# First feed-forward layer of a two-layer trunk: 288, 256 and 272 columns for its three matmul parts

## The chip, the cores and the metric

The kernel runs on one core of one Trainium2 chip. TensorE multiplies matrices, VectorE, ScalarE and GpSimd do the element-wise work, and SyncE issues the transfers. The metric is the time of one execution on the device, in microseconds.

## The reference

The reference is a decoder trunk of two layers with model width 2048 over 272 positions: 16 learned meta tokens and a sequence of 256. What matters here is the feed-forward part, once in each layer:

```python
def rmsnorm(x, g):
    y = x * lax.rsqrt(jnp.mean(x * x, axis=-1, keepdims=True) + EPS)
    return y * g

def conv_ffn(h, w_up, dw, w_down):          # D_FF = 5632
    u = causal_dwconv(h @ w_up, dw)         # width 3, causal, per channel
    val, gate = u[..., :D_FF], u[..., D_FF:]
    return (jax.nn.silu(gate) * val) @ w_down

for i in range(2):
    h = h + mixer_i(rmsnorm(h, norm_mix[i]))
    h = h + conv_ffn(rmsnorm(h, norm_ffn[i]), w_up[i], dw[i], w_down[i])
return rmsnorm(h, norm_final)[:, 16:]
```

The mixer of layer 0 is two convolution branches with a common output projection, that of layer 1 a gated linear attention and a recurrence. All inputs are float32.

## The kernel before

Positions lie along the free axis, so `h` is 16 tiles of 128 channels by 272 positions, and a matrix product for 128 output channels is a loop over k steps of 128 input channels each.

Every large product goes through `gemm_steps` (line 151). A product's weights come from memory in pieces of 8 k steps (`wf`, line 155). For 4 k steps at a time ScalarE makes the high part `wh` of the weights (line 161, a float32r cast), and VectorE (GpSimd in some products of the first mixer) the low part `wl`, what the cast left over (line 163). The moving operand is split in the same way into `xh` and `xl`. A k step is three matmuls into the same accumulator: `wh` with `xh`, `wh` with `xl`, `wl` with `xh` (lines 181 to 183). There is a second form (lines 169 to 179), used where `xs` holds triples: the positions whose low part is not multiplied apart lie in front of `xh` as additional columns, copied there from `xl`. `wh` then meets a wide operand (copied low columns, then `xh`), and the rest of `xl` in a second, narrower matmul; the accumulator's columns of the copied part are added to where they belong afterwards. In the kernel before the second form is used in the up products of layer 1 alone, with 2 such columns: 260, 256 and 258 columns. There the wide operand of the last k step is the product's last matmul.

`Norm` (line 208) makes the operand for the next products: `make_x` writes `xh` (ScalarE), `xl` (VectorE) and, where wanted, the copied columns (GpSimd, line 228) into rows of `XW` = 320 columns for the feed-forward norms and layer 0 and of 272 for the mixer of layer 1; `feed` adds up the squares, `finish` makes `rstd`, by which a product's result is multiplied afterwards.

`ffn` (line 431) runs two halves. In each, 22 pairs of up products (16 k steps each) give `val` and `gate`: the result times `rstd` into `u` (line 452), a convolution over three positions (`conv3`: ScalarE, then twice VectorE), a SiLU, a product on GpSimd (line 459), and the split into `act` (line 462), 22 tiles with rows of 320 columns in layer 0. Then 16 down products of 22 k steps each add to `h` (line 465). In layer 0 all of these have 272 columns. The tile `gap` (line 434) has no content; it shifts what is allocated behind it.

The mixer of layer 0, `mixer_ab` (line 275), ends in an output projection in two parts of 16 products with 8 k steps each (lines 415 to 427), the first over `s_split`, whose last entry is made at lines 372 to 377. In between, a layer norm written as a generator (`ln_gen`) is moved on by one step after each product. After it comes `ffn` of layer 0, the mixer of layer 1 (`mixer_cd`), `ffn` of layer 1, and the output: `ob` is scaled on VectorE and GpSimd and stored in eleven pieces from SyncE (lines 1091 to 1097). `omm` and `omka` (lines 1060 and 1061) are small constants for the mixer of layer 1, computed from the parameters on VectorE; the order on an engine is the order that the scheduler gives to instructions that don't depend on each other.

## Time and profile before

| | |
|---|---|
| median of 3 runs | 2460.76 us (2458.37, 2460.76, 2470.93) |
| the profiled execution | 2459.09 us |
| span of the profiled execution | 2457.3 us |
| TensorE busy | 2427.9 us (99%), 20476 matmuls |
| VectorE, ScalarE, GpSimd busy | 1794.0, 1338.9, 571.6 us |
| transfers | 53.0% of the 16 engines' time on the main queue |

The profile is one execution. TensorE (PE) is busy nearly all the time; VectorE is DVE, ScalarE ACT, GpSimd POOL and SyncE SP in its rows. The printed duration of a matmul is from its start to its end, and successive matmuls overlap; how far apart they start is read from their starts. The stages in order of time: mixer of layer 0 to 349 us, up and down products of layer 0 in two halves to 1132, mixer of layer 1 to 1702, up and down products of layer 1 to 2443, output.

### The profile page before, as it was taken

The numbers are of one execution on the slowest core, as the hardware profiler recorded it, in microseconds if no ns is written. First come the engines' busy times: TensorE is split into PE (matmuls) and PEld (weight loads), VectorE is DVE, ScalarE is ACT, GpSimd is POOL, SyncE is SP. The second block draws the span as 40 slices with busy tenths as digits, with TensorE's granted clock in tenths as the row PEclk, the third lists the DMA queues.
The fourth block names the chain that finished last, engine by engine and source line by source line (L and its number), as shares of the span: only waits on it lengthen the run. The fifth ranks groups of instructions, "written<-read, shape, count | busy, mean of one in ns | idle before, by whom it ended". The sixth has DMA issues, their size and how long they took to land.

```text
span 2457.3 us, 53575 instructions
## 1 busy us (share of the span) xinstructions
PE 2427.9 (99%) x20476; PEld 2371.8 (97%) x20476; DVE 1794.0 (73%) x3400; ACT 1338.9 (54%) x2573; POOL 571.6 (23%) x894
## 2 busy tenths in 40 slices
PE   8999999999999999999999999999999999999998
PEld 8999999999999999999999988899999999999997
DVE  8897897776556777667786678879777755777754
ACT  5444665555445555546745445546555545555653
POOL 5776140000000000121248044416110000101122
PEclk9999999999999999999999999999999999999999
DMA  6555555555665555665446342345555566555564
GB/s 223 191 176 180 172 173 180 181 178 173 181 183 179 178 177 180 181 196 190 142 148 179 126 130 84 101 131 179 188 184 188 183 191 197 187 184 186 179 198 147
DMA packets 130991, 423.95 MB, mean 173 GB/s; under 512 B 18832, under 2 KB 27216, under 8 KB 130736
## 3 DMA queue, kind: packets, MB, share of 16 engines
q1 hardware_dynamic: 129824, 417.99, 53.0%
q8 instruction: 161, 2.64, 0.4%
q0 software_dynamic: 912, 2.55, 0.4%
q14 instruction: 94, 0.77, 0.1%
HBM read 414.41 MB, written 5.93 MB: 171 GB/s over the span
## 4 chain that ended last, share of the span: by engine, by line
PE 97%; DVE 1%; ACT 0%; DMA 0%; issue 0%; POOL 0%; SPq 0%; DVEq 0%; POOLq 0%
PE acc L181 24%; PE acc L183 23%; PE acc L182 23%; PE acc L176 7%; PE acc L175 7%; PE acc L174 6%; PE ps L924 1%; PE ps L958 1%; PE ps L939 0%; PE acc L178 0%; PE ps L973 0%; PE ps L826 0%; PE ps L981 0%; PE ps L987 0%; DVE wl L163 0%
## 5 line engine op out<-in xcount | busy, mean ns | idle before, releaser
L161 ACT CAST wh<-wf 128x512 fp32r<-128x512 f32 (+1 forms) x1576 | 956.3, 611 | 876.4 <-PE acc L182 610.0
L163 DVE TENSOR_TENSOR wl<-wf,wh 128x512 fp32r<-128x512 f32 (+1 forms) x1465 | 1030.2, 708 | 462.6 <-ACT wh L161 417.0
L181 PE MATMUL acc<-x,wh 128*128 128x272 f32 (+2 forms) x2438 | 711.3, 292 | 1.4 <-ACT wh L161 1.4
L183 PE MATMUL acc<-x,wl 128*128 128x272 f32 (+2 forms) x2438 | 700.3, 287 | 1.0 <-DVE wl L163 0.9
L182 PE MATMUL acc<-x,wh 128*128 128x272 f32 (+2 forms) x2438 | 698.7, 287 | 0.0
L181 PEld LDWEIGHTS acc<-x,wh 128*128 128x128 f32 x2438 | 459.4, 188 | 15.7 <-issue 7.6
L183 PEld LDWEIGHTS acc<-x,wl 128*128 128x128 f32 x2438 | 459.7, 189 | 3.2 <-DVE wl L163 1.9
L182 PEld LDWEIGHTS acc<-x,wh 128*128 128x128 f32 x2438 | 459.9, 189 | 1.1 <-issue 0.3
L182 PE MATMUL acc<-act,wh 128*128 128x272 f32 (+1 forms) x1408 | 396.0, 281 | 0.0
L183 PE MATMUL acc<-act,wl 128*128 128x272 f32 (+1 forms) x1408 | 396.0, 281 | 0.0
L181 PE MATMUL acc<-act,wh 128*128 128x272 f32 (+1 forms) x1408 | 396.0, 281 | 0.0
L174 PE MATMUL acc<-x,wh 128*128 128x260 f32 x1144 | 323.6, 283 | 0.0
L176 PE MATMUL acc<-x,wl 128*128 128x258 f32 x1144 | 321.8, 281 | 0.0
L175 PE MATMUL acc<-x,wh 128*128 128x256 f32 x1144 | 321.0, 281 | 0.0
L181 PEld LDWEIGHTS acc<-act,wh 128*128 128x128 f32 x1408 | 264.7, 188 | 0.0
L183 PEld LDWEIGHTS acc<-act,wl 128*128 128x128 f32 x1408 | 264.7, 188 | 0.0
L182 PEld LDWEIGHTS acc<-act,wh 128*128 128x128 f32 x1408 | 264.7, 188 | 0.0
L175 PEld LDWEIGHTS acc<-x,wh 128*128 128x128 f32 x1144 | 215.6, 188 | 0.0
L174 PEld LDWEIGHTS acc<-x,wh 128*128 128x128 f32 x1144 | 215.5, 188 | 0.0
L176 PEld LDWEIGHTS acc<-x,wl 128*128 128x128 f32 x1144 | 215.3, 188 | 0.0
L163 POOL TENSOR_TENSOR wl<-wf,wh 128x512 fp32r<-128x512 f32 x111 | 149.0, 1350 | 55.9 <-ACT wh L161 54.8
L451 POOL MEMSET u<- 128x2 f32 x88 | 8.6, 101 | 572.9 <-DVE c L272 566.3
(334 smaller groups left out, 3740.5 us busy)
## 6 DMA issues: line engine op xcount, KB each, us to landing
wf<-up SPq DMA_DIRECT2D x352, 512.0 KB, 3.5
wf<-down SPq DMA_DIRECT2D x128, 512.0 KB, 3.8
wf<-cd_in SPq DMA_DIRECT2D x100, 512.0 KB, 3.6
wf<-ab_in SPq DMA_DIRECT2D x76, 512.0 KB, 3.6
wf<-down SPq DMA_DIRECT2D x64, 384.0 KB, 3.2
wf<-ab_out_s SPq DMA_DIRECT2D x16, 512.0 KB, 3.5
wf<-ab_out_a SPq DMA_DIRECT2D x16, 512.0 KB, 3.6
wf<-cd_out_o SPq DMA_DIRECT2D x16, 512.0 KB, 3.5
```

Of the source, the lines that this page charges most:

```text
L161: last_hi[0] = S.copy(wh[:, :ns * P], src)
L163: lo = eng.tensor_sub(wl[:, :ns * P], src, wh[:, :ns * P].bitcast(F32))
L174: PE.matmul(acc, a, x4, start=kk == 0, stop=False)
L175: PE.matmul(acc[:, 4:], a, x0, start=False, stop=False)
L176: PE.matmul(acc[:, 2:], b, x2, start=False, stop=False)
L181: PE.matmul(acc, a, xh, start=kk == 0, stop=False)
L182: PE.matmul(acc, a, xl, start=False, stop=False)
L183: PE.matmul(acc, b, xh, start=False, stop=kk == kt - 1)
L451: G.memset(u[:, 0:2], 0.0)
L924: PE.matmul(gv[:, :128], bkc, t[r, h0], start=True, stop=True)
L958: PE.matmul(wy[H[h0], 0:64], t[:, h0, 0:64], sv[:, h0], start=True, stop=True)
```

## The change

In layer 0's feed-forward part both products take the second form, with all 16 meta positions as the copied columns: 16 low columns, then the 272 high ones, make 288 for `wh`; 256 low ones; 272 high ones for `wl`. `make_x` copies 16 columns for `norm_ffn0`, and `act` gets its copy in `ffn`. The result has 288 columns: for an up product it is multiplied by `rx` (`rstd` with its first columns once more in front) into `u`, and GpSimd adds columns 0 to 15 to columns 16 to 31 and then sets two to zero for the convolution; for a down product VectorE adds the first 16 columns to `h` in a second addition. `apart` cuts the three operands so that all end at the end of a row of 320. The accumulator gets 288 columns, `gap` grows from 48 to 80.

Three further edits: the first three products of the output projection of layer 0 are interleaved (four k steps of the first and of the second, then their other four, then the third), `rstd` goes into `cv` ahead of the last product there, and `ln_gen` yields once more; `omm` and `omka` are ordered behind the last weight step of layer 0; the last stores are regrouped, and those of GpSimd's pieces are issued from ScalarE's queue.

```diff
--- before.py
+++ after.py
@@ -36,7 +36,7 @@
 TP = 320
 PAD = 48
 ACT_W = (320, 256)
-ACT_GAP = 48
+ACT_GAP = 80
 XW = 320
 NXW = KD * T // XW
 OUT = NM - 2
@@ -169,11 +169,12 @@
                     if len(xs[kk]) == 3:
 
                         x4, x0, x2 = xs[kk]
+                        e = x2.shape[-1] - SEQ
                         last = kk == kt - 1
                         if not last:
                             PE.matmul(acc, a, x4, start=kk == 0, stop=False)
-                        PE.matmul(acc[:, 4:], a, x0, start=False, stop=False)
-                        PE.matmul(acc[:, 2:], b, x2, start=False, stop=False)
+                        PE.matmul(acc[:, 2 * e:], a, x0, start=False, stop=False)
+                        PE.matmul(acc[:, e:], b, x2, start=False, stop=False)
                         if last:
                             PE.matmul(acc, a, x4, start=False, stop=True)
                         continue
@@ -184,7 +185,7 @@
                 yield
 
     def gemm(w, g, xs, n, pool_lo=()):
-        acc = psA.tile([P, T], F32, tag="acc", name="acc")
+        acc = psA.tile([P, T + 16], F32, tag="acc", name="acc")
         for _ in gemm_steps(w, g, xs, len(xs), acc[:, :n], pool_lo):
             tick()
         return acc[:, :n]
@@ -195,6 +196,10 @@
 
     def parts(t, c0, c1):
         return t[:, 0, c0:c1], t[:, 1, c0:c1]
+
+    def apart(x, n):
+        o = XW - n
+        return x[:, 0, o - (n - SEQ):], x[:, 1, XW - SEQ:], x[:, 0, o:]
 
 
     h = []
@@ -210,6 +215,7 @@
             self.g, self.c0, self.n, self.pool, self.wide = gname, c0, T - c0, pool, gname != "norm_mix1"
             self.ta, self.tb = tags
             self.x, self.acc, self.ps, self.rstd = [], None, None, None
+            self.e = {"norm_ffn0": 16, "norm_ffn1": 2}.get(gname, 0)
 
         def make_x(self, m):
             hm = h[m][:, self.c0:]
@@ -220,12 +226,13 @@
             if self.wide and m >= NXW:
                 slab, i = self.slab2, m - NXW
             x = slab[:, 2 * w * i:2 * w * (i + 1)].rearrange("p (a t) -> p a t", a=2)
-            o = XW - self.n if self.c0 else 0
+            e = self.e
+            o = XW - self.n if e else 0
             xh, xl = parts(x, o, o + self.n)
             S.activation(xh, hm, AF.Copy, scale=pc(self.g, m))
             V.scalar_tensor_tensor(xl, hm, pc(self.g, m), xh.bitcast(F32), op0=ALU.mult, op1=ALU.subtract)
-            if self.c0:
-                G.tensor_copy(x[:, 0, o - 2:o], xl[:, 0:2].bitcast(F32))
+            if e:
+                G.tensor_copy(x[:, 0, o - e:o], xl[:, 0:e].bitcast(F32))
             self.x.append(x)
 
         def feed(self, m):
@@ -252,14 +259,10 @@
             r = npool.tile([P, T], F32, tag="rstd", name="rstd", bufs=2)
             inv_sqrt(r[:, self.c0:], self.ps[:, :self.n], 1.0 / D, "eps")
             self.rstd = r[:, self.c0:]
-            if self.c0 and self.wide:
-                V.tensor_copy(r[:, self.c0 - 2:self.c0], r[:, self.c0:self.c0 + 2])
-                self.rstd = r[:, self.c0 - 2:]
 
         def xs(self):
-            if self.c0:
-                o = XW - self.n
-                return [(x[:, 0, o - 2:], x[:, 1, o + 2:], x[:, 0, o:]) for x in self.x]
+            if self.e:
+                return [apart(x, self.n) for x in self.x]
             return [parts(x, 0, self.n) for x in self.x]
 
     def add_h(m, acc, c0):
@@ -369,9 +372,9 @@
                     V.tensor_mul(up[:, 2:T + 2], u, u2)
                     cv = tp.tile([P, T], F32, tag="t2", name="cv")
                     conv3(cv, up, T, "sc_dw", i)
+                    V.tensor_mul(cv, cv, nm.rstd)
             sb = tp.tile([P, T], F32, tag="t3", name="sb")
-            V.tensor_mul(sb, ps3[2], nm.rstd)
-            V.tensor_mul(sb, sb, cv)
+            V.tensor_mul(sb, ps3[2], cv)
             d = halves[:, i]
             split(d, sb, T)
             s_split.append(parts(d, 0, T))
@@ -395,6 +398,7 @@
                     (G if i % 2 else V).tensor_add(csum, csum, sq)
                 if i % 2:
                     yield
+            yield
             pv = psb()
             PE.matmul(pv[:, :T], ones, csum, start=True, stop=True)
             yield
@@ -412,8 +416,15 @@
 
         ln = ln_gen()
         next(ln, None)
+        accs = [psA.tile([P, T + 16], F32, tag="acc", name="acc")[:, :T] for _ in range(2)] + [psb()[:, :T]]
+        heads = [gemm_steps(A["ab_out_s"], m, s_split, 8, accs[m]) for m in range(3)]
+        for i in (0, 1, 0, 1):
+            next(heads[i])
         for m in range(KD):
-            acc = gemm(A["ab_out_s"], m, s_split, T)
+            if m == 2:
+                for _ in heads[2]:
+                    pass
+            acc = accs[m] if m < 3 else gemm(A["ab_out_s"], m, s_split, T)
             h[m] = hpool.tile([P, T], F32, tag="h", name="h")
             V.tensor_add(h[m], h0[:, m], acc)
             next(ln, None)
@@ -433,10 +444,11 @@
         c0 = nm.c0
         tp.tile([P, ACT_GAP], F32, name="gap", bufs=1)
         n = T - c0
-        pad = 2 if layer == 0 else 0
+        e = nm.e
         no = n if layer == 0 else n - 2
-        ex = 0 if layer == 0 else 2
+        u0 = e - 2 if layer == 0 else e
         xs = nm.xs()
+        rx = tp.tile([P, T + 16], F32, name="rx", bufs=1)[:, :n + e]
         up, down, dw = A["up%d" % layer], A["down%d" % layer], "ffn_dw%d" % layer
         for half in range(2):
             act = []
@@ -444,25 +456,36 @@
                 i = half * NFH + j
                 res = []
                 for q in range(2):
-                    ps = gemm(up, 2 * i + q, xs, n + ex)
-                    nm.finish()
+                    ps = gemm(up, 2 * i + q, xs, n + e)
+                    if nm.rstd is None:
+                        nm.finish()
+                        V.tensor_copy(rx[:, 0:e], nm.rstd[:, 0:e])
+                        V.tensor_copy(rx[:, e:], nm.rstd)
                     u = tp.tile([P, T + 16], F32, tag="u%d" % q, name="u")
-                    if pad:
-                        G.memset(u[:, 0:2], 0.0)
-                    V.tensor_mul(u[:, pad:pad + n + ex], ps, nm.rstd)
-                    if ex:
-                        G.tensor_add(u[:, 2:4], u[:, 2:4], u[:, 0:2])
+                    V.tensor_mul(u[:, :n + e], ps, rx)
+                    G.tensor_add(u[:, e:2 * e], u[:, e:2 * e], u[:, 0:e])
+                    if layer == 0:
+                        G.memset(u[:, u0:e], 0.0)
                     c = tp.tile([P, T], F32, tag="c%d" % q, name="c")
-                    conv3(c[:, :no], u[:, ex:], no, dw, q * NF + i)
+                    conv3(c[:, :no], u[:, u0:], no, dw, q * NF + i)
                     res.append(c[:, :no])
                 silu = S.activation(res[1], res[1], AF.Silu)
                 G.tensor_mul(res[0], res[0], res[1])
-                d = tp.tile([P, 2, ACT_W[layer]], F32R, tag="act", name="act", bufs=24)
-                split(d, res[0], no)
-                act.append(parts(d, 0, no))
+                w = ACT_W[layer]
+                d = tp.tile([P, 2, w], F32R, tag="act", name="act", bufs=24)
+                split(d[:, :, w - no:], res[0], no)
+                if no > SEQ:
+                    G.tensor_copy(d[:, 0, w - no - e:w - no], d[:, 1, w - no:w - SEQ].bitcast(F32))
+                    act.append(apart(d, no))
+                else:
+                    act.append(parts(d, 0, no))
             warm(AF.Sqrt, [silu])
+            ea = no - SEQ
             for m in range(KD):
-                add_h(m, gemm(down, half * KD + m, act, no), T - no)
+                acc = gemm(down, half * KD + m, act, no + ea)
+                add_h(m, acc[:, ea:], T - no)
+                if ea:
+                    V.tensor_add(h[m][:, 0:ea], h[m][:, 0:ea], acc[:, 0:ea])
                 if half:
                     feed(nxt, m)
                     if spill is not None:
@@ -1057,8 +1080,11 @@
 
     omm = cpool.tile([P, 26], F32, name="omm")
     omka = cpool.tile([P, 16], F32, name="omka")[:, :8]
-    V.tensor_scalar(omm, par[:, PO["mu"]:PO["mu"] + 26], -1.0, 1.0, op0=ALU.mult, op1=ALU.add)
-    V.tensor_scalar(omka, par[:, PO["ka"]:PO["ka"] + 8], -1.0, 1.0, op0=ALU.mult, op1=ALU.add)
+    late = last_lo[0]
+    o1 = V.tensor_scalar(omm, par[:, PO["mu"]:PO["mu"] + 26], -1.0, 1.0, op0=ALU.mult, op1=ALU.add)
+    o2 = V.tensor_scalar(omka, par[:, PO["ka"]:PO["ka"] + 8], -1.0, 1.0, op0=ALU.mult, op1=ALU.add)
+    for o in (o1, o2):
+        behind(o, [late])
     with tc.tile_pool(name="cd", bufs=2) as tp:
         nm = mixer_cd(tp, nm)
     with tc.tile_pool(name="ffn1", bufs=2) as tp:
@@ -1088,13 +1114,13 @@
             PE.matmul(ps[:, P * i:P * i + P], rw[:, i], cc("ident", P), start=True, stop=True)
         rs = tp.tile([P, SEQ], F32, name="rs", bufs=1)
         S.copy(rs, ps[:, :SEQ])
-        for a, b in ((0, 1), (1, 2), (11, 12), (2, 4), (12, 13), (4, 6), (13, 14), (6, 8), (14, 15), (8, 11), (15, 16)):
+        for a, b in ((0, 1), (11, 12), (1, 3), (12, 13), (3, 5), (13, 14), (5, 7), (14, 15), (7, 9), (15, 16), (9, 11)):
             for m in range(a, b):
                 if m < 11:
                     V.tensor_mul(ob[:, m], ob[:, m], ps[:, :SEQ])
                 else:
                     G.tensor_mul(ob[:, m], ob[:, m], rs)
-            nc.sync.dma_start(A["outT"][:, a:b], ob[:, a:b])
+            (nc.sync if a < 11 else nc.scalar).dma_start(A["outT"][:, a:b], ob[:, a:b])
```

## Rows read from the trace of the kernel before

**Rows 1.** The page: busy time, share, instructions; granted clock in 40 slices.

```profile
PE 2427.9 (99%) x20476; PEld 2371.8 (97%) x20476; DVE 1794.0 (73%) x3400; ACT 1338.9 (54%) x2573; POOL 571.6 (23%) x894
...
PEclk9999999999999999999999999999999999999999
```

**Rows 2.** By stretch: us, busy (x instructions) of each engine; clock, DMA share, GB/s.

```profile
349.00:609.00 260.00, 260.00 (x2109) 259.92 (x2108) 185.92 (x331) 145.03 (x265) 20.83 (x68) 1.00 0.54 177
...
1000.00:1132.00 132.00, 132.00 (x1085) 131.36 (x1087) 87.99 (x134) 67.38 (x118) 28.04 (x30) 1.00 0.67 192
...
1702.00:1952.00 250.00, 250.00 (x2105) 249.94 (x2104) 187.39 (x331) 149.10 (x265) 25.38 (x66) 1.00 0.56 184
```

**Rows 3.** TensorE by line, six stretches: count, ns min/median/max, first, last start.

```profile
L181 PE MATMUL acc<-x,wh x556: 285/288/288, 745.8 to 997.8; 128*128 128x272 f32 x186
...
L181 PE MATMUL acc<-lt,wh x128: 285/285/288, 745.1 to 994.1; 128*128 128x272 f32 x128
...
L181 PE MATMUL acc<-act,wh x309: 285/285/288, 610.8 to 724.7; 128*128 128x272 f32 x155
...
L181 PE MATMUL acc<-act,wh x340: 276/276/276, 1954.7 to 2070.0; 128*128 128x256 f32 x170
...
L175 PE MATMUL acc<-x,wh x548: 276/281/284, 1710.1 to 1949.9; 128*128 128x256 f32 x183
...
L175 PE MATMUL acc<-lt,wh x126: 276/281/284, 1712.6 to 1946.9; 128*128 128x256 f32 x126
...
L181 PE MATMUL acc<-ysp,wh x121: 281/283/287, 1657.0 to 1700.2; 128*128 128x258 f32 x121
...
L181 PE MATMUL acc<-x,wh x46: 283/288/291, 1274.0 to 1290.9; 128*128 128x272 f32 x46
```

**Rows 4.** TensorE's waits in two stretches: engine line <- releaser: us, times, longest.

```profile
PE ps L251 <- DVE sum L307: 2.1, 1, 2.1
...
PE acc L182 <- DVE halves L194: 1.9, 1, 1.9
```

**Rows 5.** Timeline of VectorE, 28 to 31 us: start, us, engine line op.

```profile
28.50 1.25 DVE L1060 TENSOR_SCALAR omm<-par 128x26 f32<-128x26 f32 x1
...
29.74 1.50 DVE L307 TENSOR_TENSOR sum<-sum,sum 128x272 f32<-128x272 f32 x1
```

**Rows 6.** Timeline of VectorE, 251 to 257 us.

```profile
251.11 0.44 DVE L373 TENSOR_TENSOR sb<-acc,rstd 128x272 f32<-128x272 f32 x1 [0.20 <-PE acc L183]
...
252.29 1.01 DVE L374 TENSOR_TENSOR sb<-sb,cv 128x272 f32<-128x272 f32 x1
...
253.22 1.93 DVE L391 TENSOR_TENSOR conv<-conv,mu 128x272 f32<-128x272 f32 x2
...
255.07 0.99 DVE L194 TENSOR_TENSOR halves<-sb,halves 128x272 fp32r<-128x272 f32 x1
```

**Rows 7.** The tail: timeline of VectorE and GpSimd, and the stores.

```profile
2447.48 3.73 DVE L1094 TENSOR_TENSOR ob<-ob,ps 128x256 f32<-128x256 f32 x11 [1.41 <-ACT rs L1090]
...
2447.53 3.46 POOL L1096 TENSOR_TENSOR ob<-ob,rs 128x256 f32<-128x256 f32 x5 [8.68 <-ACT rs L1090]
...
L1097 SPq DMA_DIRECT2D outT<-ob x11: 343/400/448, 2448.3 to 2453.1; - x11
...
DMA to landing us min/median/max: 1.7/2.2/2.7
```

**Rows 8.** Groups by form of the nearest small operations: busy, mean ns, idle.

```profile
L454 POOL TENSOR_TENSOR u<-u 128x2 f32<-128x2 f32 x88 | 18.4, 209 | 475.1 <-DVE u L452 475.1
...
L228 POOL CAST x<-x 128x2 fp32r<-128x2 f32 x13 | 8.4, 646 | 0.7 <-DVE x L226 0.7
...
L266 DVE TENSOR_TENSOR h<-h,acc 128x272 f32<-128x272 f32 x48 | 20.6, 429 | 0.5 <-PE acc L183 0.5
```

**Rows 9.** Timeline at the first half's last `act`: VectorE and TensorE.

```profile
614.40 0.44 DVE L194 TENSOR_TENSOR act<-c,act 128x272 fp32r<-128x272 f32 x1 [1.99 <-ACT act L193]
...
617.43 0.28 PE L181 MATMUL acc<-act,wh 128*128 128x272 f32 x1
```

## The prediction, made before the change was run

> **What bounds the kernel now.** I read the page's first part, then the clock row, then the waits of TensorE, then the stages one by one. [rows 1]: TensorE is busy for 2427.9 of 2457.3 us and its granted clock is the upper of its two levels, 2.4 GHz, from end to end, so no clock is to be won back. [rows 2]: in the stretch of the first feed-forward layer's up projection TensorE is busy 260.00 of 260.00 us while VectorE has 186 and GpSimd 21; the second layer's up projection, where the form of matmul that the change brings in already stands, looks the same (250.00 of 250.00, GpSimd 25). So in these stages the time is the number of matmuls times the distance from one matmul's start to the next one's. The printed duration of a matmul (0.28 us) is no help, since they overlap; the distance is.
>
> I take the distance from rows that give a count with the first and the last start [rows 3]. One k step is three matmuls (weights high with x high, high with x low, low with x high), and one line holds one of the three, so the distance between two instructions of that line is a k step:
> - layer 0 up, three times 272 columns: (997.8 - 745.1) / 683 = 370.0 ns (556 + 128 instructions);
> - layer 0 down, also 272: (724.7 - 610.8) / 308 = 369.8;
> - layer 1 down, three times 256: (2070.0 - 1954.7) / 339 = 340.1;
> - layer 1 up, 260, 256 and 258 columns: (1949.9 - 1710.1) / 673 = 356.3 (548 + 126);
> - the second half of the output projection of layer 1, three times 258: (1700.2 - 1657.0) / 120 = 360.0;
> - the input projection of layer 1, three times 272, from a slab 272 wide: (1290.9 - 1274.0) / 45 = 375.6, plus or minus 2 as the starts are rounded to 0.1 us.
>
> Only few places make TensorE wait: 2.1 us for the sum of squares at the beginning and 1.9 us for `halves` before the output projection of layer 0 [rows 4]. And behind the last matmul there is a tail in which the output is scaled and stored [rows 7].
>
> **The change, part 1: the matmuls.** A k step of layer 0 keeps its three matmuls and its 816 columns: 3 x 272 becomes 288 + 256 + 272. At 2.4 GHz 816 columns are 340 ns, and [rows 3] show 370.0, so 30 ns of each k step are something else, and the question is whether the new shapes carry less of it. In clock periods (0.4167 ns) a 272 matmul takes 296, which is 272 + 24; a 256 matmul takes 272, which is 256 + 16. I tried a simple rule on the rows: 16 periods for each matmul, and 8 more for each stretch of 64 columns (256 bytes) that its moving operand covers only in part (a piece under 8 columns counts as 8). Rows of 320 = 5 x 64 columns, as `x` and `act` have here, start on such a stretch. The rule is my estimate, made on two of the rows; the other three test it. Input projection of layer 1: the slab's width of 272 puts starts at 0, 16, 32 and 48 within a stretch, half of the steps take 896 periods and half 904, together 375.0 ns (row: 375.6). 258 columns: 868 periods, 361.7 ns (row: 360.0). Layer 1 up: 260 from column 60 and 258 from column 62 end on a stretch and take 288 each, 256 from column 64 takes 272; 848 periods, 353.3 ns (row: 356.3). So the three rows lie 0.6 above, 1.7 below and 3.0 above the rule.
>
> For the new k step: 288 columns from column 32 are half a stretch and four whole ones, 288 + 24 = 312; the 256 from column 64 are four whole ones, 272; the 272 from column 48 are 296. Sum 880 periods, 366.7 ns, or 3.3 below the present 370.0. Layer 0 has 88 up products of 16 k steps (1408) and 32 down products of 22 (704): 2112 x 3.33 ns = **7.0 us gained**. By the rule's own misses the k step may be 365.0 to 369.7, so 10.6 down to 0.6 us. I take the 7.0: the row with the largest miss has pieces of 2 and 4 columns, and the new pieces are 16 and 32, as in the input projection where the rule holds.
>
> A rule that speaks against this part: the Trainium skill (TensorE: Matmul & The Clock Gate, section "Wait — 56ns, not 53.3ns?") gives a warm matmul its columns at 2.4 GHz plus a fixed 2.5 ns or so. By that, equal columns cost equal time and part 1 is worth nothing. The trace does not agree in the step that matters: from 256 to 272 columns a matmul grows by 10.0 ns [rows 3], where that rule would give 6.7.
>
> **Part 2: the work around the matmuls.** All of it lies beside a TensorE that is full, and I cost it at nothing. Each of the 88 up products gains one GpSimd add of 16 columns (0.21 us in its two-column form), in front of the convolution on ScalarE; each of the 44 pairs one GpSimd cast of 16 columns (0.65 us for two) [rows 8]. A pair of products lasts 2 x 16 x 0.37 = 11.8 us, of which GpSimd now fills 0.95 (20.83 us for 22 pairs [rows 2]) and then some 2. ScalarE now waits for that add before the convolution, and behind it are queued the weight casts; layer 1 has this wait already, with TensorE at 250.00 of 250.00 [rows 2]. The 32 down products gain a VectorE add of 16 columns, bounded by the 0.43 us of the 272 form [rows 8], in 8.1 us each. The place with least cover is the last `act` of a half: it is complete at 614.84 and TensorE comes to its first matmul on it at 617.43 [rows 9]. The new chain adds the GpSimd add (0.2) and a memset of two columns before the convolution and the cast (0.65) behind the split, about 1 us of 2.6. Were that cover gone, the cost would be the excess, twice. In the new form the matmul that reads the copied columns is also the last of its product. The norm's 16 new casts (0.65 us each) run during the output projection, before the 5.5 us in which the first up product gets to its last k.
>
> **Part 3: moved steps.** (a) `omm` and `omka` stand in VectorE's queue between the sums of squares and the last sum for which TensorE waits. They hold the queue from 28.50 to 29.74 [rows 5], and the last sum ends at 31.24, which is where TensorE goes on. Sent behind the last weight step of layer 0, they leave 1.24 us: **1.2 us gained**. There VectorE has idle time (88.0 of the 132 us of that stretch busy [rows 2]), and their readers come later. (b) Before the layer-0 output projection TensorE stops for 1.9 us at k 7, as `halves` comes at 256.06 [rows 6]. The change does four more k steps first (1.5 us), and takes `rstd` into `cv` beforehand, so that the 1.01 us product goes out of the chain and the 0.44 us one does both. 1.5 + 1.0 is more than 1.9, and next late is nothing that the waits show: **1.9 us gained**, with 1.5 if VectorE's two `conv` subtractions (1.93 us [rows 6]) still come in between. The weight transfers on SyncE keep their order, one a product; only the second product's is wanted 1.5 us sooner, and its casts on ScalarE and VectorE with it. The additional step in the layer norm's generator moves one small matmul by one product and costs nothing. (c) The tail: the eleven stores go out one behind the other on SyncE, the first at 2448.3 and the last at 2453.1, 0.48 us apart, while VectorE is done at 2451.21 and GpSimd at 2450.99 [rows 7]. With five of them on ScalarE's queue, which is idle then, the last leaves SyncE 0.4 us after VectorE's last multiply, about 2451.6 in place of 2453.1; it carries 256 KB in place of 128, and landings take 1.7 to 2.7 us [rows 7]. So **1.5 us gained**, with bounds 0 (if ScalarE's issues, which the trace doesn't show, take turns with SyncE's) and 1.7.
>
> The sum: 7.0 + 1.2 + 1.9 + 1.5 = 11.6 us. The profiled execution took 2459.1 us as a whole, 1.8 around its span, and the median of the runs is 2460.8. That gives 2447.5 on the one and 2449.2 on the other; I forecast 2448.6.
>
> **The rivals.**
> - *Columns alone count.* The 30 ns beside the columns belong to the three instructions and not to their shapes, and the k step stays within 1 ns of 370. For: the total of columns is the same, and layer 1 up lies 3.0 above my rule, which would nearly undo the 3.3. Against: 256 to 272 grows by 10 ns. Only part 3 is left: 2460.8 - 4.6 = 2456, some 2454 to 2458. The Trainium skill's rule cited above would have it so.
> - *Slower: the mixed form has a price of its own.* Between matmuls of unequal width and operand start, each step may lose time that uniform ones don't. Layer 1 up carries 356.3 ns for 774 columns, 0.4603 a column; at that rate 816 columns take 375.6, or 5.6 more than now, 11.8 us over 2112 steps, less 4.6 from part 3: 2468. It decides from 372.2 ns for a k step, where part 3 is eaten up. Against: that row is still 3.7 below three times 258.
> - *More than forecast.* If a piece at the front of an operand costs nothing because it ends on a whole stretch, each matmul takes its columns + 16: 864 periods, 360.0 ns, 21 us gained, 2435 in all. Against: layer 1 up would be at 342.5, not 356.3.
> - *The change doesn't reach the down products.* `act` lies behind tiles whose sizes change; if its rows began 48 columns off a stretch, the first matmul would have 8 periods more, the second 16, the third 8: 912, 380 ns, 7.0 us lost over 704 steps where 2.3 was to be won. With 4.7 won in the up products and 4.6 in part 3 that is 2458.5. Against: the gap grows by 32 and a tile of 288 comes in, together 320, five whole stretches.
>
> **How the numbers follow.** Forecast 0.55 (2446 to 2451), columns alone 0.22, slower 0.09, more 0.07, down products not reached 0.07. Half a per cent (12.3 us, to 2448.5 or 2473) is about what a measurement of this kernel can tell from no change, and the forecast lies on that edge: I give two fifths of it (0.22) and all of "more" to faster, and add 0.05 for terms that are each a little larger; of the slower case, 0.05 reaches 2473. So faster 0.34, same 0.61, slower 0.05. The range takes in the forecast, "columns alone" and the down case, and leaves out the slower case and most of "more": 2443 to 2459.
>
> **What would show it.** The distance of the line with the 288 columns should be 366.7 ns in both stages of layer 0; TensorE's waits should lose the entry for `halves` and 1.2 us of that for the sum; the last store should leave by 2451.7. A k step above 370, a wait of TensorE for `act` at the head of a down product, or one for the copied columns of `x`, would make the prediction wrong.

## The result: 0.7% slower, and the profile after

| | before | after |
|---|---|---|
| median of 6 runs each, beside one another | 2460.47 us (2458.37 to 2470.93) | 2478.88 us (2477.19 to 2480.22) |
| ratio, 95% interval | | 1.0072 [1.0061, 1.0084] |
| span of the profiled execution | 2457.3 us | 2477.3 us |

The change costs 15 to 21 us where a gain of 12 was forecast; the time lies above the range. First the page of the kernel after: its busy times and the granted clock, as in [rows 1].

```profile
PE 2448.2 (99%) x20476; PEld 2391.0 (97%) x20476; DVE 1809.4 (73%) x3435; ACT 1343.4 (54%) x2573; POOL 604.7 (24%) x1042
...
PEclk9999999999999999999999999999999999999999
```

As many matmuls as before, the upper clock level throughout, and TensorE is busy 20.3 us longer while the span grew by 20.0. So it isn't waiting: its matmuls stand further apart. The first matmul of each stage says where:

| stage | starts at, before | after | length, before | after |
|---|---|---|---|---|
| layer 0 up, first half | 348.72 | 348.17 | 260.94 | 267.55 |
| layer 0 down, first half | 609.66 | 615.72 | 130.24 | 133.65 |
| layer 0 up, second half | 739.90 | 749.37 | 260.48 | 267.23 |
| layer 0 down, second half | 1000.38 | 1016.60 | 132.30 | 136.03 |
| mixer of layer 1 | 1132.68 | 1152.63 | | |

The four stages whose matmuls were changed lose 6.6 + 3.4 + 6.8 + 3.7 = 20.5 us. The mixer of layer 1 (569.0 us up to its feed-forward part) and layer 1's up products (251.4) are as long as before. In the profile the loss is read from the line of the 256-column matmul, which stands once in every k step (the columns are line, operation, count, ns min/median/max, first and last start). The line in a down stage, then in an up stage:

```profile
L176 PE MATMUL acc<-act,wh x316: 279/283/283, 620.0 to 739.6; 128*128 128x256 f32 x158
```

```profile
L176 PE MATMUL acc<-x,wh x546: 279/283/283, 755.6 to 1009.1; 128*128 128x256 f32 x182
L176 PE MATMUL acc<-lt,wh x127: 281/283/283, 754.8 to 1009.9; 128*128 128x256 f32 x127
```

(739.6 - 620.0) / 315 = 379.7 ns and (1009.9 - 754.8) / 672 = 379.6, where [rows 3] had 370.0. Over 2112 k steps 9.7 ns are 20.5 us, the whole loss. A settled k step in the middle of a product takes 380 (starts to the nanosecond). A stretch of the timeline (start, us, engine, line) shows how a k step divides:

```profile
500.84 0.28 PE L176 MATMUL acc<-x,wh 128*128 128x256 f32 x1
500.96 0.29 PE L177 MATMUL acc<-x,wl 128*128 128x272 f32 x1
501.08 0.30 PE L175 MATMUL acc<-x,wh 128*128 128x288 f32 x1
501.22 0.28 PE L176 MATMUL acc<-x,wh 128*128 128x256 f32 x1
```

In starts to the nanosecond, from a matmul's start to the next one's, the 256 takes 118.1, the 272 127.9 and the 288 133.3 (means over 245 us of the first up stage); before, each of the three took 123.3.

The work beside the matmuls stays hidden. The first up stage of layer 0 by window (columns as in [rows 2]):

```profile
350.00:615.00 265.00, 265.00 (x2096) 264.92 (x2096) 191.59 (x330) 147.11 (x262) 35.54 (x129) 1.00 0.52 173
```

TensorE is busy for 265.00 of 265.00 us with GpSimd at 35.54 instead of 20.83. Of the waits of [rows 4] both are gone. What stands there now (TensorE from 20 to 350 us; us, times, longest) is new except for the 0.5 us, which the kernel before has as well:

```profile
PE acc L184 <- DVE wl L163: 1.4, 1, 1.4
PE acc L182 <- ACT wh L161: 0.9, 1, 0.9
PE ps L184 <- DVE wl L163: 0.5, 1, 0.5
PE acc L184 <- POOL wl L163: 0.2, 1, 0.2
```

And the tail, against [rows 7]:

```profile
2467.84 3.73 DVE L1120 TENSOR_TENSOR ob<-ob,ps 128x256 f32<-128x256 f32 x11 [1.72 <-ACT rs L1116]
```

```profile
L1123 SPq DMA_DIRECT2D outT<-ob x6: 332/344/717, 2468.3 to 2471.6; - x6
L1123 ACTq DMA_DIRECT2D outT<-ob x5: 338/380/893, 2468.6 to 2471.4; - x5
...
DMA to landing us min/median/max: 1.7/2.8/4.4
```

The last store leaves 3.8 us behind the first multiply (before 5.6), but the slowest landing takes 4.4 us (before 2.7).

### The profile page after: what moved, and what is told of

It reads as the page before. It is cut to its first block, busy times and chain, and to the rows that moved or that the text cites. A ratio compares the mean times of both kernels' runs of the same rounds, so it can differ in the third digit from the quotient of the medians.

```text
span 2477.3 us, 53767 instructions
## 1 busy us (share of the span) xinstructions
PE 2448.2 (99%) x20476; PEld 2391.0 (97%) x20476; DVE 1809.4 (73%) x3435; ACT 1343.4 (54%) x2573; POOL 604.7 (24%) x1042
## 4 chain that ended last, share of the span: by engine, by line
PE 95%; DVE 2%; DMA 1%; ACT 1%; POOL 0%; issue 0%; SPq 0%; DVEq 0%; ACTq 0%; POOLq 0%
PE acc L177 17%; PE acc L175 17%; PE acc L176 17%; PE acc L182 13%; PE acc L184 12%; PE acc L183 12%; PE acc L179 1%; PE ps L947 1%; DVE ps L319 1%; PE ps L981 1%; DVE wl L163 0%; PE ps L962 0%; PE ps L996 0%; PE ps L849 0%; PE ps L1004 0%
## 5 line engine op out<-in xcount | busy, mean ns | idle before, releaser
L175 PE MATMUL acc<-x,wh 128*128 128x288 f32 (+1 forms) x2288 | 663.2, 290 | 0.0
L177 PE MATMUL acc<-x,wl 128*128 128x272 f32 (+1 forms) x2288 | 653.5, 286 | 0.0
L176 PE MATMUL acc<-x,wh 128*128 128x256 f32 x2288 | 644.1, 282 | 0.0
L182 PE MATMUL acc<-x,wh 128*128 128x272 f32 (+2 forms) x1294 | 382.7, 296 | 1.7 <-ACT wh L161 1.7
L184 PE MATMUL acc<-x,wl 128*128 128x272 f32 (+2 forms) x1294 | 372.1, 288 | 2.5 <-DVE wl L163 2.4
L183 PE MATMUL acc<-x,wh 128*128 128x272 f32 (+2 forms) x1294 | 370.5, 286 | 0.0
L466 POOL TENSOR_TENSOR u<-u 128x16 f32<-128x16 f32 (+1 forms) x176 | 38.9, 221 | 926.3 <-DVE u L465 926.3
L177 PE MATMUL acc<-act,wl 128*128 128x272 f32 x704 | 202.8, 290 | 0.0
L175 PE MATMUL acc<-act,wh 128*128 128x288 f32 x672 | 199.5, 297 | 0.0
L176 PE MATMUL acc<-act,wh 128*128 128x256 f32 x704 | 197.8, 283 | 0.0
L183 PE MATMUL acc<-act,wh 128*128 128x256 f32 x704 | 194.3, 276 | 0.0
L184 PE MATMUL acc<-act,wl 128*128 128x256 f32 x704 | 194.3, 276 | 0.0
L182 PE MATMUL acc<-act,wh 128*128 128x256 f32 x704 | 194.3, 276 | 0.0
```

The lines of the kernel that those rows point to most:

```text
L175: PE.matmul(acc, a, x4, start=kk == 0, stop=False)
L176: PE.matmul(acc[:, 2 * e:], a, x0, start=False, stop=False)
L177: PE.matmul(acc[:, e:], b, x2, start=False, stop=False)
L182: PE.matmul(acc, a, xh, start=kk == 0, stop=False)
L183: PE.matmul(acc, a, xl, start=False, stop=False)
L184: PE.matmul(acc, b, xh, start=False, stop=kk == kt - 1)
```

## The experiments

Four theories stood beside the rule of the prediction. W: a matmul grows by 1.5 periods for each column above 256, whatever its start and neighbours. S: an operand that begins inside a stretch of 64 columns costs time. D: the place in the accumulator to which a matmul writes (columns 0, 32 and 16 here) costs time. M: unequal neighbours cost something that equal ones don't. The k step is the measure in all of them.

**1. Uniform shapes.** All k steps but the first and the last of a product take three matmuls of one shape, another shape in each stage. The four numbers of a matmul are the part of the operand (0 high, 1 low), the column where it starts, its width, and the column of the accumulator to which it writes.

```diff
+    FORMS = {
+        ('up', 0, 0): ((0, 32, 288, 0), (0, 32, 288, 0), (0, 32, 288, 0)),
+        ('up', 0, 1): ((0, 48, 272, 0), (1, 48, 272, 0), (0, 48, 272, 0)),
...
+                        if FORM[0] and 0 < kk < kt - 1:
+                            x = xs[kk][3]
+                            for (part, o, wd, dst), lhs in zip(FORM[0], (a, a, b)):
+                                PE.matmul(acc[:, dst:dst + wd], lhs, x[:, part, o:o + wd], start=False, stop=False)
+                            continue
```

> In each half of the feed-forward products of layer 0, and in the up products of layer 1, the three matmuls of all k steps but the first and last of a product get one shape, so these products are not those of the reference; the number of matmuls stays. With W = columns, start = column of the row of 320 where the moving operand begins, to = column of the accumulator where the result begins: layer 0 up first half 3 x W 288 start 32 to 0; up second half 3 x W 272 start 48 to 0; down first half 3 x W 256 start 64 to 0; down second half 3 x W 272 start 48 to 16; layer 1 up first half 260, 256, 258 from 60, 64, 62 all to 0; up second half 3 x W 258 start 62 to 0. Theory W (a matmul grows by 1.5 periods a column above 256, whatever its neighbours): 400.0 ns a k step for 288, 370 for 272 everywhere, 340 for 256. Theory rule of the prediction (8 periods for a stretch covered in part): 390, 370, 340, 370, 353 to 356, 360. Theory D (a result that begins inside the accumulator costs time): down second half well above 370, by some 10 ns, layer 1 up first half at 353 or below, the rest as the rule. Theory S (an operand that begins inside a stretch costs time): up second half at 375 or more and layer 1 up second half above 360. Theory M (unequal neighbours cost time): everything uniform at the rule's values, layer 1 up first half unchanged at 356.

Measured, ns for three: 288 from column 32 395.2; 272 from 48 379.8, and 379.9 with its results to column 16 (so D falls); 256 from 64 340.5; 258 from 62 359.6; layer 1's three shapes with all results to column 0 356.3, as in [rows 3]. The down product of 256 columns, by one of its lines, the first and the last of 20 k steps:

```profile
640.38 0.28 PE L187 MATMUL acc<-act,wl 128*128 128x256 f32 x1
...
646.84 0.28 PE L187 MATMUL acc<-act,wl 128*128 128x256 f32 x1
```

6.46 / 19 = 340.0. So the 272 alone is 10 ns above the row of before: there its operand started at column 0, here at 48. The rule had both at 296 periods. W had 400 for the 288 and 370 for the 272, and M left both at the rule's 390 and 370, so neither is enough; S had asked for 375 or more for the 272, and its other sign, 258 from 62 above 360, did not come.

What the 356.3 is made of changes the reading of [rows 3]. It is no steady distance but the mean of two, here and in the kernel before: there every third product of the layer 1 up stage runs at 353.3 and the two behind it at 357.7. The 256-column line of two successive products of the kernel before:

```profile
1719.71 0.28 PE L175 MATMUL acc<-x,wh 128*128 128x256 f32 x1
...
1723.95 0.28 PE L175 MATMUL acc<-lt,wh 128*128 128x256 f32 x1
```

```profile
1725.37 0.28 PE L175 MATMUL acc<-x,wh 128*128 128x256 f32 x1
...
1730.02 0.28 PE L175 MATMUL acc<-lt,wh 128*128 128x256 f32 x1
```

4.24 us over 12 k steps are 353.3 ns, 4.65 over 13 are 357.7. The prediction's rule gave 353.3, which a third of the products meet and two thirds miss.

**2. The change's mix, and mixes of 256.** The same edit with other forms: the change's three operands with all results to column 0; in the order 288, 272, 256; 256 columns from unlike starts.

```diff
+        ('up', 0, 0): ((0, 32, 288, 0), (1, 64, 256, 0), (0, 48, 272, 0)),
+        ('up', 0, 1): ((0, 32, 288, 0), (0, 48, 272, 16), (1, 64, 256, 32)),
+        ('down', 0, 0): ((0, 32, 256, 0), (1, 64, 256, 0), (0, 48, 256, 0)),
```

> As the run with uniform shapes, but with mixed ones; these products are not those of the reference. Layer 0 up first half: the change's operands (288, 256, 272 from 32, 64, 48), all to column 0 of the accumulator: theory D 366.7 ns a k step, theories W, S and M 380. Up second half: the change's three matmuls in the order 288, 272, 256: 380 if the order plays no part; another value under M. Down first half: 3 x 256 from 32, 64, 48, all to 0: theory S well above 353, the rule and M 353, D 353, W alone 340. Down second half: 3 x 256 from 64, to 0, 32 and 16: theory D some 350 or more, all others 340. Layer 1 up first half: 3 x 256 from 64, to 0, 4 and 2: D some 343, others 340. Layer 1 up second half: 3 x 256 from 60, 64, 62, all to 0: S above 355, rule 355, W alone 340.

Measured: 380.0 with all results to column 0 (the first three products 376.6); 376.8 in the other order; 356.4 for 256 columns from 32, 64 and 48, as the mean of 353.4 in every third product and 358.2 in the others; 340.5 for 256 from 64 to three different accumulator columns; 355.4 for 256 from 60, 64 and 62, where 353.8 and 356.9 take turns. The change's mix to column 0, two rows of one product:

```profile
482.07 0.29 PE L187 MATMUL acc<-x,wl 128*128 128x272 f32 x1
...
487.01 0.29 PE L187 MATMUL acc<-lt,wl 128*128 128x272 f32 x1
```

4.94 / 13 = 380.0. The destination costs nothing; start and order do.

**3. The other edits alone.** The kernel before with `omm` and `omka` late, the interleaved heads with `rstd` in `cv`, and the regrouped stores; it keeps its own three times 272.

```diff
+        heads = [gemm_steps(A["ab_out_s"], m, s_split, 8, accs[m]) for m in range(3)]
+        for i in (0, 1, 0, 1):
+            next(heads[i])
...
+            (nc.sync if a < 11 else nc.scalar).dma_start(A["outT"][:, a:b], ob[:, a:b])
```

> The kernel before with the further edits alone (interleaved first products of the output projection and rstd taken into cv, the constants behind the last weight step, the regrouped stores). If my terms for them hold: 4.6 us below the kernel before. If what the changed kernel's trace shows holds for them (the projection's end 0.5 us earlier, the tail 0.4 us shorter): about 1 us below, within the noise of the measurement. The matmuls of layer 0 at 370.0 ns a k step under both.

Measured: median 2457.60 us (2455.73 to 2459.68, 10 runs), ratio 0.9983 [0.9973, 0.9992], which is 2.0 to 6.6 us faster. That holds the forecast 4.6 and not the 1; the spans of the two profiled executions differ by 1.5 (2457.3 and 2455.8). This version beats both kernels. Its waits in the mixer, then its stores:

```profile
PE acc L181 <- ACT wh L161: 0.9, 1, 0.9
PE ps L183 <- DVE wl L163: 0.5, 1, 0.5
PE acc L183 <- POOL wl L163: 0.2, 1, 0.2
```

```profile
L1108 SPq DMA_DIRECT2D outT<-ob x6: 332/344/978, 2447.0 to 2450.4; - x6
L1108 ACTq DMA_DIRECT2D outT<-ob x5: 338/374/869, 2447.4 to 2450.1; - x5
...
DMA to landing us min/median/max: 1.8/2.8/3.8
```

The 1.4 us wait for `wl` of the changed kernel isn't among them; it stands in that one execution. But there is a loss that no wait shows, in the output projection. One line of it, up to 290 us and behind:

```profile
L183 PE MATMUL acc<-halves,wl x55: 285/288/288, 269.8 to 289.7; 128*128 128x272 f32 x55
```

```profile
L183 PE MATMUL acc<-halves,wl x152: 289/290/290, 290.4 to 347.8; 128*128 128x272 f32 x152
```

19.9 / 54 = 369 ns, then 57.4 / 151 = 380. Nothing of the shapes differs. Between them the timeline has one short stop:

```profile
289.74 0.29 PE L183 MATMUL acc<-halves,wl 128*128 128x272 f32 x1
290.09 0.36 PE L181 MATMUL acc<-halves,wh 128*128 128x272 f32 x1
```

**4. The copied columns behind the high part.** The change as it is, but `xh` at the front of its row and the 16 copied columns behind it, so that the operands start at 0 (288), 64 (256) and 0 (272).

```diff
+        if n == T:
+            return x[:, 0, :T + 16], x[:, 1, XW - SEQ:], x[:, 0, :T]
```

> The change with the 16 copied columns behind the high part and not before it: operands 288 from 0, 256 from 64, 272 from 0, results to 0, 16 and 0; the same sums, added back from the end of the accumulator. Theory S: no operand begins inside a stretch, 366.7 ns a k step, some 28 us below the changed kernel, 2451. Theory W: 320 + 272 + 296 = 888 periods, 370.0 ns, 2459. Theory D: one result of three still begins inside, 371 to 375. Theory M: 380 as in the changed kernel, 2479.

Measured: median 2466.81 us (2464.33 to 2469.31, 10 runs), ratio 1.0025 [1.0015, 1.0034]: 12 us better than the change, and still slower than before. The line of its 256 columns in the second up stage:

```profile
L178 PE MATMUL acc<-x,wh x533: 279/280/280, 754.8 to 998.5; 128*128 128x256 f32 x178
L178 PE MATMUL acc<-lt,wh x123: 279/280/281, 759.7 to 999.5; 128*128 128x256 f32 x123
```

244.7 / 655 = 373.6 ns. Of the 10.0 ns, 6.5 are the starts; 3.5 stay with aligned ones. No theory alone has this value but D (371 to 375), and D fell in the first two experiments: S had 366.7, W 370.0, M 380.

**5 and 6. Two maps.** In the up products of layer 0 the inner 14 k steps take one of 22 forms each, four products a form.

```diff
+            FORM[0] = FORMS[(2 * i + q) // 4]
```

> In the up products of layer 0 the three matmuls of all k steps but the first and last of a product take one of 22 forms, four products of each form one after the other, all but the last form from the high part of x and to column 0 of the accumulator; these products are not those of the reference. Equal forms: width 256 from column 0, 16, 32, 48, 64 of the row, 272 from 0, 16, 32, 48, 288 from 0, 16, 32. Then unequal ones, as width from start: 288,256,272 all from 0; 288,272,256 from 0; 288,288,256 from 0; 288,256,256 from 0; 272,256,256 from 0; 272,272,256 from 0; 272 from 0,48,0; 272 from 48,0,48; the change's 288 from 32, 256 from 64, 272 from 48 to column 0; the change as it is. Theory S (each matmul has a price by its width and by where its operand begins, and prices add up): 256 from 64 113.3 ns a matmul, 272 from 0 123.3, 272 from 48 126.6, 288 from 32 131.7 as already seen; 256 from 16, 32 or 48 some 118 to 122; 288 from 0 some 130; each unequal form the mean of its three equal ones, so 288,256,272 from 0 at 367 a k step and the change near 372. Theory M (unequal neighbours cost time beside that): the unequal widths from 0 above the mean of their equal forms by 6 ns or more a k step, the one with 288,272,256 less so, the change at 380; 272 from 0,48,0 at the mean of its equals, 372. Theory W (1.5 periods a column above 256, whatever the start): 288 from 0 133.3, 288,256,272 from 0 at 370.

> Made like the first map: 22 forms of the three matmuls in the up products of layer 0, four products each, from the high part of x and to column 0 of the accumulator (these products are not those of the reference). Equal forms: width 258, 260, 264, 268, 276, 280, 284 from column 0, 256 from 8, 272 from 8 and from 24. Unequal, as width from start: 288 from 0, 256 from 64, 272 from 0; 288/32, 256/64, 272/0; 288/0, 256/64, 272/48; 288/32, 256/64, 272/48; 288/32, 256/64, 272/32; 288/32, 272/48, 256/64; 288/0, 272/0, 256/64; 272/48, 272/48, 256/64; 272/0, 272/0, 256/64; 288/32, 288/32, 256/64; 260/60, 256/64, 258/62; 260/0, 256/0, 258/0. Theory S+M (price by width and start, and 256 costs 117.8 ns and not 113.3 beside wider ones): from the first map's prices 288/0 133.3, 288/32 131.7, 272/0 123.3, 272/48 126.7, the six forms of the change's widths 374, 373, 378, 376, 376, 376; 272/48 twice and 256 371; 272/0 twice and 256 364 to 367; 288/32 twice and 256 381. The starts decide the change's loss if 288/32, 256/64, 272/0 lies at 374 or below and 288/32, 256/64, 272/48 at 380. Theory M alone (widths decide, starts don't matter among unequal widths): all six within 2 ns of one another. Theory W for the widths: 1.5 periods a column above 256 and 16 beside them give 114.6, 115.8, 118.3, 120.8 for 258, 260, 264, 268 and 125.8, 128.3, 130.8 for 276, 280, 284; the rule of the prediction gives 116.7 for 258 and 264, 118.3 for 260 at most, 121.7 for 268, then 125.0, 126.7, 128.3.

| ns for three matmuls | start 0 | 16 | 32 | 48 | 64 |
|---|---|---|---|---|---|
| 256 columns | 340.0, one product 353.3 | 359.5 | 340.2 and 353.3 | 360, last two 356 | 340.7, one 353.3 |
| 272 | 370.0 | 375.4 to 376.1 | 380.0 | 380.0 | |
| 288 | 400.0 | 395.0 | 395.0 | | |

| mixed k step (columns/start) | ns | mean of its shapes among their equals (256 at 340) |
|---|---|---|
| 288/0, 256/0, 272/0 | 373.5 | 370.0 |
| 272/0, 256/0, 256/0 | 357.5 | 350.0 |
| 272/0, 272/48, 272/0 | 373.7 | 373.3 |
| 288/0, 288/0, 256/0 | 379.9 | 380.0 |
| 288/0, 256/64, 272/48 | 373.3 | 373.3 |
| 288/32, 256/64, 272/0 | 374.7, settled 373.3 | 368.3 |
| 288/32, 256/64, 272/48 (the change) | 380.0 | 371.7 |

What mixed forms take above the mean runs from nothing to 8.3 ns: S alone, which adds up prices, had nothing, and M 6 or more for unequal widths. The rows behind four of these: 272 from 0, 272 from 48, 288 from 0, and 288, 256, 272 from 0 (start, us, engine, line; the last column is the count of instructions that a row holds):

```profile
460.82 0.41 PE L203 MATMUL acc<-x,wh 128*128 128x272 f32 x2
...
465.88 0.29 PE L203 MATMUL acc<-lt,wl 128*128 128x272 f32 x1
...
532.97 0.42 PE L203 MATMUL acc<-x,wh 128*128 128x272 f32 x2
...
538.16 0.29 PE L203 MATMUL acc<-lt,wl 128*128 128x272 f32 x1
...
557.26 0.42 PE L203 MATMUL acc<-x,wh 128*128 128x288 f32 x2
...
562.73 0.29 PE L203 MATMUL acc<-lt,wl 128*128 128x288 f32 x1
...
772.61 0.41 PE L203 MATMUL acc<-x,wh 128*128 128x288 f32 x2
...
777.70 0.29 PE L203 MATMUL acc<-lt,wl 128*128 128x272 f32 x1
```

Each pair is the first and the last start of one product's 42 inner matmuls, 41 distances: 5.06, 5.19 and 5.47 us are 123.4, 126.6 and 133.4 ns for one matmul, so 370, 380 and 400 for three; 5.09 us are 372.4 for the mixed one, which ends on its last matmul (by starts of one line, once settled, 371 and 376 in turn: 373.5).

The second map has widths from column 0, for three: 258 360 to 362, 260 360, 264 362, 268 373 (one product of four 379.5), 276 380, 280 385, 284 400 (one 393.3). So the cost climbs by uneven steps, and most of them lie inside a stretch of 64 columns.

## Why the prediction was wrong

**The step that failed is part 1**, the rule of 16 periods a matmul and 8 for each partly covered stretch of 64 columns. It gave 880 periods for the new k step; settled, it takes 912 (380.0 ns). By matmul:

| | by the rule | measured in the change |
|---|---|---|
| 288 from column 32 | 312 periods, 130.0 ns | 133.3 ns |
| 256 from column 64 | 272, 113.3 | 118.1 |
| 272 from column 48 | 296, 123.3 | 127.9 |

Three errors, 3.3, 4.8 and 4.6 ns, make 12.7. The right column is means over the whole first up stage, 379.3 in sum; the settled 380.0 would make 13.3.

- *The width.* Among equals and from column 0, 256, 272 and 288 take 113.3, 123.3 and 133.3 ns. The steps are equal. The 288 gives back exactly what the 256 saves, 133.3 + 113.3 + 123.3 = 370.0: even without any price for mixing there was nothing to gain. The rule let the last 16 columns cost 16 periods (6.7 ns) where they cost 24; no row of [rows 3] had 288 columns, and the prediction extended the rule there with no bound but the rule's misses on narrower shapes.
- *The mix.* With all starts on a multiple of 64 the mix takes 373.5, not 370.0. The 256 has a second steady value among equals too, 353.3 for three or 117.8 each, and in most mixes with wider shapes it takes 116 to 118. With 117.8 for it the sum is 374.4, 0.9 above what was measured. Unequal neighbours don't always bring that: in 288/0, 256/64, 272/48 the 256 takes 112.6 to 114.2, and the whole is the mean of its equals. What decides between the two values is open. Price: 3.5 x 2112 = 7.4 us.
- *The starts.* 272 from column 48 takes 126.7 ns, from 0 123.3. The rule gave both the same, as it counts stretches and not where an operand begins. Its test on the input projection of layer 1, 0.6 ns off, was no test: starts 0, 16, 32 and 48 take turns there (0 and 32, the high part, twice as often), and the mean of the measured 370, 376, 380 and 380 with these weights is 376.0, inside the row's plus or minus 2 like the rule's 375.0. In the change two operands begin inside a stretch. Moving either of them to a multiple of 64 gives 373.3 to 374.7, both together 373.5 to 373.8: among these widths the price isn't a sum over operands, though among three times 272 it is (373.7 for 0, 48, 0). Nor is the aligned start always the cheaper one: the 288 among its equals takes 400 from 0 and 395 from 16 or 32. The price of the starts is 6.5 x 2112 = 13.7 us, and the fourth kernel got back 12.

Together 21.1 us if every k step were a settled one; the four stages lost 20.5. Less the 2.0 to 6.6 of the other edits that is 13.9 to 18.5, against 15.0 to 20.7 by the ratio.

**The rivals.** It went as the slower one said, a price of the mixed form, at 380.0 ns where it had 375.6; a chance of 0.09 was low for it, and its 375.6 was worked out from the 356.3 that is a mean of two distances. The argument against it, that layer 1's mix lies 3.7 below three times 258, compared the wrong things: its own shapes from column 0 take 359.3, from 60, 64 and 62 353.3 or 357.7, and 256 among its equals can take 340 or 353. "Columns alone" falls: three layouts of the same 816 columns took 370.0, 373.5 and 380.0. The rule of the Trainium skill by which it would have come so (TensorE: Matmul & The Clock Gate, section "Wait — 56ns, not 53.3ns?", columns at 2.4 GHz and 2.5 ns more) doesn't agree with these rows: by it 256 and 288 columns differ by 13.3 ns, measured are 20.0. "The change doesn't reach the down products" isn't it either, as up and down both take 380; its 912 periods were the right number for another reason.

**Part 2 was right.** No wait of TensorE for `act` or the copied columns stands in the profile.

**Part 3 was right in its waits and not in what they gave.** (a) The wait for `sum` is gone, and in the third kernel the projection starts at 249.59 instead of 251.16, 1.6 us where 1.2 was forecast. The changed kernel's execution had a wait of 1.4 us for `wl` at 58.6 us instead and starts it at 251.34. (b) The wait for `halves` is gone, but the third product now waits 0.9 us for its first weight cast on ScalarE: what was next late, which the prediction found in no row. From the projection's first matmul to the first up product it is 97.56 us before, 96.83 after: 0.7 gained of 1.9. In the third kernel it is 98.34, as 152 k steps at 380 instead of 370 lose 1.5. (c) The last store left 1.9 us sooner, but landings grew; from the first multiply to the end of the span it is 9.8 us before, 9.5 after (2477.3 - 2467.84) and 9.2 in the third kernel, so 0.3 to 0.6 for the 1.5 that the forecast took from the issue alone.

**What stays open**: why an operand's start and unequal neighbours move the distance of matmuls, and why one form has two steady values. No run here separates the reading of the operand from the loading of the weights.

## What to carry to other kernels

An equal total of columns is not equal time: price each shape by its width, the column its operand starts at and its neighbours, from the starts of a steady stretch, product by product, as a mean can hide two distances. A rule fitted to a few rows must be tested on rows with one start and one width each, and a shape outside those rows gets bounds from both sides; one run that steps through many forms, four products each, settles what no argument did. Of the arrangements of 288, 256 and 272 tried here none settled under 373; three times 272 from column 0 at 370 is the better form, and the other edits are worth keeping without the new one.

## What the runs showed of the hardware that was not expected

- The cost of a matmul climbs unevenly with its width: from column 0, 120.0 ns at 260 columns, 120.7 at 264, 124.4 at 268, 126.7 at 276, 128.3 at 280, 133.3 at 284 and 133.3 at 288 (one product of four at 268 took 126.5, one at 284 131.1).
- One form can run at two distances, with nothing changed in it: the layer 1 up k step at 353.3 in every third product and 357.7 in the others; three times 256 from column 0 at 340.0 or 353.3 in successive products, and three times 272 from column 0 at 370 up to a stop that puts two starts 350 ns apart, and at 380 for the next 57 us. In the first experiment's execution the same projection also went over from 370 to 380; in those of before and of the change it stayed at 370. So about 1.5 us come and go with an execution here.
- The column of the accumulator to which a matmul writes costs nothing: 272 to columns 0 and 16 took 379.8 and 379.9.
- Stores on two issuing queues left sooner and landed later: the slowest landing took 2.7 us before, 4.4 in the changed kernel and 3.8 in the third.
